# Weight sums of the down projection kept in a DRAM scratch in a one-layer decoder step

## The chip, the cores and the metric
One core of one Trainium2 chip runs the whole program. The metric is the device time of one execution in microseconds (us), lower is better. The engines are TensorE (PE in the profile), VectorE (DVE), ScalarE (ACT), GpSimd (POOL) and SyncE (SP), which issues all the DMA transfers named here.

## The reference, cut to what matters
```python
def _layer(x, ...):                       # 1024 prompt + 64 sample tokens, D_MODEL = 1024
    ...                                   # input projection, attention, S5, output projection
    h = x + mixed
    hn = rmsnorm(h, norm2_g)
    y = h + (jax.nn.silu(hn @ w_gate) * (hn @ w_up)) @ w_down    # D_FF = 2816, float32
    return y, ...
```
A final RMSNorm with `final_norm_g` follows. The change concerns the last product, with `w_down` (2816 x 1024).

## The kernel before, in words
All 1088 tokens go through one layer. The last third of the time is the feed-forward block (`phase_e`): first gate and up (`ffn`), then the down projection (`down`). Tokens lie in two halves `t` of 2 x 272 columns.

Float32 products are made from two parts of each operand: `split` (L63 to L65) writes the high part with ACT (L64) and the rest, source minus high part, with DVE (L65) or, for some tiles, with POOL. `mm3` (L68 to L72) then does three matmuls of 128x128 weights on 272 columns.

Both stages use Strassen's scheme with seven products `j` for each 2x2 block, and so sums of weight blocks. In gate and up a step is one product for both token halves, 8 groups of three matmuls; from its second group of columns on there are 140 such steps. `wsums` (L1615) makes three of the weight sums on POOL when a unit's weights have landed, `wpart` (L1624) a fourth at j = 3; `wsplit` then splits the 128x512 block for the step, LA = 3 steps ahead of its product, into a ring `ws` of 5 buffers.

In `down` a unit is (t, d, u): token half, 256 output columns, and a third of the 2816 rows. Units u = 0 and 1 have seven Strassen steps of 12 matmuls, u = 2 has six steps of plain products, whose one difference is made in `sums` (L1755). So each (t, d) has 20 steps, and there are 160 in all. `load(i)` fetches the raw weights of the next unit at its predecessor's first step, `sums(i + 1)` makes its sums on POOL at the third step. Both token halves use the same weights: they are loaded and summed twice. The hidden activations come back from DRAM (`hs<-dH`, `xp<-dH`, in `fill` and `plain`) and are split as well: 14 tiles of 128x1088 and four of 128x816 at the start of each token half, one per step (`cut`). Further work of POOL here: the base sums (L1794) and the scaling of finished rows (L1887).

The order on each engine's queue is worked out when the program is built, by a scheduler that goes by readiness and program order; on the chip each queue then runs in that fixed order. Loads and stores all stand in SP's queue.

Of the kernel before, what the change touches and what calls it, by code (L numbers as in the profile page):

```python
# [10 lines left out]
F32 = mybir.dt.float32  # L11
# [3 lines left out]
OP = mybir.AluOpType  # L15
# [31 lines left out]
class K:  # L47
# [1286 lines left out]
    def phase_e(self):  # L1334
        nc, I, O = self.nc, self.I, self.O
        V = nc.vector
        with ExitStack() as st:
# [4 lines left out]
            wp = E(self.pool("wpE", 1))  # L1342
# [21 lines left out]

            dH = [[self.dram.tile([7, 128, 4, HW] if u < 2 else [4, 128, 3, HW], F32, name=f"dH{t}{u}") for u in range(3)] for t in range(2)]
            dy = [self.dram.tile([2 * HW, 1024], F32, name=f"dy{t}") for t in range(2)]
            fs = ExitStack()
            fh = fs.enter_context(self.pool("fh", 1))
            fz = fs.enter_context(self.pool("fz", 1))
# [215 lines left out]

            self.cuts, self.step = [], 0
            HS = {}
            for step in ffn:
                self.cut()
                for s in step:  # L1590
                    self.fill(HS, dH, hnew, 0, *s)
                next(side, None)
# [31 lines left out]
    def wpart(self, R, S, j):  # L1624
        (a, b), (s1, s2) = R, S
        if j == 3:
            self.nc.gpsimd.tensor_tensor(out=s2, in0=b[:, :, 0:128], in1=s2, op=OP.subtract)  # L1627
        return (a[:, :, 0:128], s2, b[:, :, 0:128], a[:, :, 128:256], s1, s2, b[:, :, 128:256])[j]


    def ffn(self, wp, fp, X, dH, wraw, wsplit, htile, stile, ttile):
        nc, I = self.nc, self.I
        V, G = nc.vector, nc.gpsimd
        P = NF // 2
        mats = [(p, m, (t,)) for p in (0,) for t in range(2) for m in "gu"]
        mats += [(p, m, (0, 1)) for p in range(1, P) for m in "gu"]
        R, S, W = {}, {}, {}

        def load(i):
            if i < len(mats):  # L1640
                p, m, _ = mats[i]
                w = I["ffn_w_gate" if m == "g" else "ffn_w_up"][0][:, 256 * p:256 * p + 256].rearrange("(k p) c -> p k c", p=128)
                R[i] = [wraw(), wraw()]
                for h in range(2):
                    self.load(R[i][h], w[:, 4 * h:4 * h + 4])

        def sums(i):
            if i < len(mats):
                S[i] = self.wsums(wp, R[i], 4)

        def prep(n):
            i, j = divmod(n, 7)
            if i < len(mats):
                W[n] = wsplit(self.wpart(R[i], S[i], j))
        load(0)
        yield
        sums(0)
        load(1)
        yield
        for n in range(LA):  # L1660
            prep(n)
        yield
        yield
        st, hid = {}, {}
        for n in range(7 * len(mats)):
            i, j = divmod(n, 7)
            p, m, tps = mats[i]
            if j == 0:
                load(i + 1) if i else None
            elif j == 2:  # L1670
                sums(i + 1)
            prep(n + LA)
            for t in tps:
                z = st.setdefault((i, t), {})
                z[j] = self.bank("mm")[:, :HW]
                x = X[t][XN[j]]
                for kt in range(4):
                    self.mm3(z[j], W[n][:, 0, kt], W[n][:, 1, kt], x[:, 0, kt], x[:, 1, kt], kt == 0, kt == 3)
                if j == 0:
                    z["r"] = ttile("t1", "r")  # L1680
                    nc.scalar.activation(z["r"], z[0], AF.Copy)
                    continue
                if j == 1:
                    z["u2"] = ttile("t2", "u2")
                    V.tensor_tensor(z["u2"], z["r"], z[1], op=OP.add)
                    continue
                if j == 3:
                    z["u3"] = ttile("t3", "u3")
                    V.tensor_tensor(z["u3"], z["u2"], z[3], op=OP.add)
                    continue  # L1690
                if j == 2:
                    z["s" if m == "g" else "o"] = stile() if m == "g" else htile("hid")
                s = z["s"] if m == "g" else st[i - 1, t]["s"]

                mt, tt = {2: (0, 0), 4: (1, 1), 5: (0, 1), 6: (1, 0)}[j]
                sb = s[:, 2 * mt + tt]
                o = sb if m == "g" else z["o"][:, mt, HW * tt:HW * tt + HW]
                u = {2: z["r"], 4: z.get("u3"), 5: z.get("u4"), 6: z.get("u3")}[j]
                V.tensor_tensor(o, u, z[j], op=OP.subtract if j == 6 else OP.add)  # L1699
                if j == 4:  # L1700
                    z["u4"] = ttile("t1", "u4")
                    V.tensor_tensor(z["u4"], z["u2"], z[4], op=OP.add)
                if m == "g":
                    nc.scalar.activation(sb, sb, AF.Silu)
                    continue
                G.tensor_tensor(out=o, in0=o, in1=sb, op=OP.mult)  # L1706
                strassen = p < 8
                ob = z["o"].rearrange("p m (c t) -> p (m c) t", c=2)
                if j == 5 and strassen:
                    z["x"] = htile("x").rearrange("p m (c t) -> p (m c) t", c=2)  # L1710
                    for out, b, c in ((z["x"][:, 0], 1, ob[:, 0]), (z["x"][:, 1], 3, z["x"][:, 0]), (ob[:, 1], 3, ob[:, 1])):
                        G.tensor_tensor(out=out, in0=ob[:, b], in1=c, op=OP.subtract)
                if j == 6:
                    d = dH[t][p // 4][:, :, p % 4].rearrange("a p t -> p a t")
                    self.store(d[:, 0:4], ob)
                    if strassen:
                        G.tensor_tensor(out=z["x"][:, 2], in0=ob[:, 2], in1=z["x"][:, 1], op=OP.subtract)
                        self.store(d[:, 4:7], z["x"][:, 0:3])
            yield [(0, j)] + [(1, k) for k in range(7) if j == 6] if p == P - 1 and m == "u" else ()
# [4 lines left out]
    def down(self, wp, dp, HS, dh, dH, dy, wraw, wsplit, hnew):  # L1724
# [2 lines left out]
        wd = I["ffn_w_down"][0]  # L1727
        units = [(t, d, u) for t in range(2) for d in range(4) for u in range(3)]
        steps = [(i, j) for i in range(len(units)) for j in range(7 if units[i][2] < 2 else 6)]
        R, S, W, HO, GF = {}, {}, {}, {}, {}  # L1730
        SS = [dp.tile([128, 6, 4 + t], F32, name=f"ss{t}") for t in range(2)]
        G.memset(SS[1], 1.0)

        def load(i):
            if i < len(units):
                t, d, u = units[i]
                n = 4 if u < 2 else 3
                w = wd[1024 * u:1024 * u + 256 * n, 256 * d:256 * d + 256].rearrange("(q h p) c -> h p q c", h=2, p=128)
                R[i] = [wraw()[:, :n] for h in range(2)]
                for h in range(2):  # L1740
                    self.load(R[i][h], w[h])
                if u == 1:
                    HO[t, d] = self.dpx[2].tile([128, 2, 2 * HW], F32, tag="o", name="o", bufs=2)
                    self.load(HO[t, d], dh[t][d].rearrange("a p t -> p a t"))
                    GF[t, d] = dp.tile([128, 256], F32, tag="gf", name="gf", bufs=1)
                    self.load(GF[t, d], I["final_norm_g"].unsqueeze(0)[:, 256 * d:256 * d + 256].to_broadcast((128, 256)))

        def sums(i):
            if i < len(units):
                if units[i][2] < 2:  # L1750
                    S[i] = self.wsums(wp, R[i], 4)
                else:
                    S[i] = [wp.tile([128, 4, 128], F32, tag="st", name="st", bufs=2)[:, :3] for h in range(2)]
                    for h in range(2):
                        G.tensor_tensor(out=S[i][h], in0=R[i][h][:, :, 0:128], in1=R[i][h][:, :, 128:256], op=OP.subtract)  # L1755

        def prep(n):
            if n < len(steps):
                i, j = steps[n]
                if units[i][2] < 2:  # L1760
                    W[n] = wsplit(self.wpart(R[i], S[i], j))
                else:
                    w, h = divmod(j, 2)
                    W[n] = wsplit(S[i][h] if w == 2 else R[i][h][:, :, 128 * w:128 * w + 128], 3)

        def plain(t, c):
            for h in range(2):
# [2 lines left out]
                self.cuts.append((self.step, x[:, 0], x[:, 1], raw(x[:, 1]), G if (h, c) in PPOOL else None))  # L1770
        tail = iter(())
        load(0)
        for c in range(2):
            plain(0, c)
        sums(0)
        for n in range(LA):
            prep(n)
        for n, (i, j) in enumerate(steps):
            t, d, u = units[i]
            if j == 0:  # L1780
                load(i + 1)
                if u == 0:
                    z = {k: self.bank("mm")[:, :HW] for k in (0, 1, 3, 2, 4, 6, 5)}
            elif j == 2:
                sums(i + 1)
            prep(n + LA)
            self.cut()
            next(tail, None)
# [187 lines left out]
```

## Time and profile before
| | |
|---|---|
| median of 3 runs | 1586.97 us (1584.7 to 1587.9) |
| profiled execution | 1586.99 us, span 1585.2 us |
| busy: PE, DVE, POOL, ACT | 1451.3, 1156.9, 890.2, 718.1 us |
| gate and up, steady part | about 900 to 1276 us of the span |
| down projection | about 1276 to 1572 us of the span |

Times in rows are us from the span's start, unless ns is written. A busy PE is not PE at its peak; the number of matmuls in a stretch tells how fast it went. A time behind an instruction holds all that it waits for once it has started.

### The profile page before, as it was taken

The numbers are of one execution on the slowest core, as the hardware profiler recorded it, in microseconds if no ns is written. First come the engines' busy times: TensorE is split into PE (matmuls) and PEld (weight loads), VectorE is DVE, ScalarE is ACT, GpSimd is POOL, SyncE is SP. The second block draws the span as 40 slices with busy tenths as digits, with TensorE's granted clock in tenths as the row PEclk, the third lists the DMA queues.
The fourth block names the chain that finished last, engine by engine and source line by source line (L and its number), as shares of the span: only waits on it lengthen the run. The fifth ranks groups of instructions, "written<-read, shape, count | busy, mean of one in ns | idle before, by whom it ended". The sixth has DMA issues, their size and how long they took to land.

```text
span 1585.2 us, 27784 instructions
## 1 busy us (share of the span) xinstructions
PE 1451.3 (92%) x9909; PEld 1348.1 (85%) x9909; DVE 1156.9 (73%) x2178; ACT 718.1 (45%) x1831; POOL 890.2 (56%) x807
## 2 busy tenths in 40 slices
PE   6988988889999999899869999999999989988896
PEld 5978978867777677789859999999999979977896
DVE  6895489858757777688898555555555597799685
ACT  6233434345476766764444323233333453454343
POOL 3069445337635465555678656555553395678672
PEclk9998988859669999799989999999999999999998
DMA  8438888697775762633314332223332473384654
GB/s 218 155 132 286 239 245 228 195 230 191 200 199 162 200 180 80 177 99 109 110 40 129 104 103 91 83 88 89 92 102 82 147 269 122 127 305 142 185 156 121
DMA packets 213464, 246.20 MB, mean 155 GB/s; under 512 B 26798, under 2 KB 164878, under 8 KB 213326
## 3 DMA queue, kind: packets, MB, share of 16 engines
q1 hardware_dynamic: 213326, 244.43, 52.4%
q8 instruction: 78, 1.28, 0.4%
q14 instruction: 60, 0.49, 0.1%
HBM read 184.43 MB, written 59.95 MB: 154 GB/s over the span
## 4 chain that ended last, share of the span: by engine, by line
PE 58%; DVE 21%; DMA 8%; issue 5%; POOL 3%; ACT 3%; SPq 1%; DVEq 0%; POOLq 0%; ACTq 0%
PE pmm L72 14%; PE pmm L70 14%; PE pmm L71 14%; PE psd L75 7%; PE pmm L75 4%; DVE ws L65 4%; PE ppo L75 2%; PE ptr L79 2%; DMA kk<-in_cache_attn_k_dram 2%; DVE hT L1545 1%; DVE hn L65 1%; DVE hs L65 1%; DVE kk L680 1%; DVE Sm L687 1%; DMA wr<-in_w_in_dram 1%
## 5 line engine op out<-in xcount | busy, mean ns | idle before, releaser
L70 PE MATMUL pmm<-hn,ws 128*128 128x272 f32 x1232 | 359.3, 292 | 9.3 <-DVE s L1699 6.4
L72 PE MATMUL pmm<-hn,ws 128*128 128x272 f32 x1232 | 358.2, 291 | 3.1 <-DVE ws L65 3.1
L71 PE MATMUL pmm<-hn,ws 128*128 128x272 f32 x1232 | 357.9, 291 | 2.5 <-DVE hn L65 2.5
L65 DVE TENSOR_TENSOR ws<-wr,ws 128x512 fp32r<-128x512 f32 (+2 forms) x240 | 258.1, 1084 | 35.4 <-ACT ws L64 34.7
L70 PEld LDWEIGHTS pmm<-hn,ws 128*128 128x128 f32 x1232 | 234.3, 190 | 10.2 <-issue 7.7
L71 PEld LDWEIGHTS pmm<-hn,ws 128*128 128x128 f32 x1232 | 234.6, 190 | 3.1 <-DVE hn L65 3.1
L72 PEld LDWEIGHTS pmm<-hn,ws 128*128 128x128 f32 x1232 | 234.0, 190 | 3.6 <-DVE ws L65 3.4
L64 ACT ACTIVATE ws<-wr 128x512 fp32r<-128x512 f32 (+2 forms) x240 | 152.2, 642 | 173.8 <-PE pmm L72 165.9
L65 DVE TENSOR_TENSOR ws<-st,ws 128x512 fp32r<-128x512 f32 (+1 forms) x136 | 132.2, 975 | 82.9 <-ACT ws L64 82.0
L64 ACT ACTIVATE ws<-st 128x512 fp32r<-128x512 f32 (+1 forms) x136 | 83.6, 616 | 134.4 <-PE pmm L72 98.5
L72 PE MATMUL pmm<-hs,ws 128*128 128x272 f32 x448 | 133.3, 298 | 8.6 <-DVE ws L65 7.9
L70 PE MATMUL pmm<-hs,ws 128*128 128x272 f32 x448 | 132.4, 296 | 4.6 <-DVE hid L1699 4.3
L71 PE MATMUL pmm<-hs,ws 128*128 128x272 f32 x448 | 132.0, 295 | 0.1
L1619 POOL TENSOR_TENSOR st<-wr 128x512 f32<-128x512 f32 x40 | 56.7, 1417 | 102.0 <-DVE ws L65 101.2
L1706 POOL TENSOR_TENSOR hid<-hid,s 128x272 f32<-128x272 f32 x88 | 82.0, 938 | 43.7 <-DVE hid L1699 43.7
L826 POOL TENSOR_TENSOR vs<-vr,vs 128x512 fp32r<-128x512 f32 x40 | 55.6, 1398 | 86.5 <-ACT vs L824 75.0
L1627 POOL TENSOR_TENSOR st<-wr,st 128x512 f32<-128x512 f32 x40 | 57.8, 1444 | 80.3 <-DVE ws L65 80.3
L679 POOL TENSOR_TENSOR kf<-kf,qb 128x1024 f32<-128x1024 f32 x24 | 61.5, 2570 | 67.6 <-DMA kf<-in_cache_attn_k_dram 54.4
L72 PEld LDWEIGHTS pmm<-hs,ws 128*128 128x128 f32 x448 | 85.9, 192 | 11.4 <-DVE ws L65 11.3
L70 PEld LDWEIGHTS pmm<-hs,ws 128*128 128x128 f32 x448 | 86.3, 193 | 5.2 <-issue 4.5
L71 PEld LDWEIGHTS pmm<-hs,ws 128*128 128x128 f32 x448 | 86.3, 193 | 0.3 <-DVE hs L65 0.3
L1123 DVE CUSTOM_DVE_ANT_0 P<-pmm,lnc 128x256 f32<-128x256 f32 (+1 forms) x128 | 47.6, 377 | 52.7 <-PE pmm L75 42.2
(438 smaller groups left out, 4193.8 us busy)
## 6 DMA issues: line engine op xcount, KB each, us to landing
vr<-in_cache_attn_v_dram SPq DMA_DIRECT2D x80, 256.0 KB
wr<-in_ffn_w_down_dram SPq DMA_DIRECT2D x32, 512.0 KB
hs<-dH SPq DMA_DIRECT2D x28, 544.0 KB
kf<-in_cache_attn_k_dram SPq DMA_DIRECT2D x48, 256.0 KB
wr<-in_ffn_w_gate_dram SPq DMA_DIRECT2D x24, 512.0 KB
wr<-in_ffn_w_up_dram SPq DMA_DIRECT2D x24, 512.0 KB
dH<-hid SPq DMA_DIRECT2D x22, 544.0 KB
wr<-in_w_in_dram SPq DMA_DIRECT2D x16, 512.0 KB
```

Of the source, the lines that this page charges most:

```text
L64: self.nc.scalar.activation(hi, src, AF.Copy)
L65: (eng or self.nc.vector).tensor_tensor(out=lo, in0=src, in1=raw(hi), op=OP.subtract)
L70: nc.tensor.matmul(out, lhsT=wh, rhs=xh, start=start, stop=False)
L71: nc.tensor.matmul(out, lhsT=wh, rhs=xl, start=False, stop=False)
L72: nc.tensor.matmul(out, lhsT=wl, rhs=xh, start=False, stop=stop)
L75: self.nc.tensor.matmul(out, lhsT=w, rhs=x, start=start, stop=stop)
L679: nc.gpsimd.tensor_tensor(out=kf[i], in0=kf[i], in1=qb[b][:, 0:1].to_broadcast((128, 2, 512)), op=OP.mult)
L826: eng.tensor_tensor(out=s[:, 1], in0=vr[i], in1=raw(s[:, 0]), op=OP.subtract)
L1123: V.tensor_tensor_reduce(out=P[h, g].rearrange("p b k -> p (b k)")[:, o:o + n], in0=s[:, o:o + n], in1=lnc[:, part, 256 - n:256], scale=-1 ...
L1619: G.tensor_tensor(out=s1, in0=a[:, :, 128:256], in1=b[:, :, 128:256], op=OP.add)
L1627: self.nc.gpsimd.tensor_tensor(out=s2, in0=b[:, :, 0:128], in1=s2, op=OP.subtract)
L1706: G.tensor_tensor(out=o, in0=o, in1=sb, op=OP.mult)
```

## The change
The seven (or, for u = 2, six) weight blocks of each unit are made once, before `down`, and kept in four DRAM tensors `dS`, one for each `d`. A generator `stationary` does it in 24 pieces, two for each (u, d). A piece loads its raw weights in four loads of 128x256 (u = 2: two), makes its sums on POOL with four instructions of 128x256 (u = 2: one of 128x384), and stores them with four stores (u = 2: two). A piece is traced at every fifth step of gate and up from step 39 to step 154, and its POOL instructions are placed behind `self.mark`, the last product `hid` made on POOL so far. In `down`, `load`, `sums` and `wpart` no longer touch weights; `wload(k)` reads the finished blocks of two steps (4 KB for each partition where both are Strassen steps) in one load, six pairs ahead, into a ring of seven buffers (four of the old `wr`, three new `wx`).

```diff
+            self.dS = [self.dram.tile([128, 74, 128], F32, name=f"dS{d}") for d in range(4)]
...
-            for step in ffn:
+            dwp = fs.enter_context(self.pool("dw", 1))
+            stat = self.stationary(dwp)
+            for n, step in enumerate(ffn):
                 self.cut()
+                if n > 35 and n % 5 == 4:
+                    with self.tc.issue_after(self.mark):
+                        next(stat, None)
...
+    def stationary(self, dw):
...
+        for u in range(3):
+            for d in range(4):
+                o = self.dS[d]
+                for x in range(2):
+                    R = dw.tile([128, 2, 2, 2, 128], F32, tag="dr", name="dr", bufs=2)
+                    S = dw.tile([128, 3, 2, 128], F32, tag="ds", name="ds", bufs=2)
+                    if u == 2:
...
+                        for k in range(2):
+                            self.load(R[:, 3 * k:3 * k + 3], w[x, k])
+                        G.tensor_tensor(out=S, in0=R[:, 0:3], in1=R[:, 3:6], op=OP.subtract)
+                        o2 = o[:, 56:74].rearrange("p (w h q) c -> p w h q c", w=3, h=2)
+                        self.store(o2[:, 0:2, x], R.rearrange("p (w q) c -> p w q c", w=2))
+                        self.store(o2[:, 2, x], S)
+                    else:
...
+                        for h in range(2):
+                            for k in range(2):
+                                self.load(R[:, h, k], w[h, k])
+                        G.tensor_tensor(out=S[:, 1], in0=R[:, 0, 1], in1=R[:, 1, 1], op=OP.add)
+                        G.tensor_tensor(out=S[:, 0], in0=S[:, 1], in1=R[:, 0, 0], op=OP.subtract)
+                        G.tensor_tensor(out=S[:, 2], in0=R[:, 1, 0], in1=S[:, 0], op=OP.subtract)
+                        G.tensor_tensor(out=R[:, 0, 1], in0=R[:, 0, 0], in1=R[:, 0, 1], op=OP.subtract)
+                        o7 = o[:, 28 * u:28 * u + 28].rearrange("p (j q) c -> p j q c", q=4)[:, :, 2 * x:2 * x + 2]
+                        self.store(o7[:, 0:4:3], R[:, 0])
+                        self.store(o7[:, 2:7:4], R[:, 1])
+                        self.store(o7[:, 1], S[:, 0])
+                        self.store(o7[:, 4:6], S[:, 1:3])
+                    yield
...
-                G.tensor_tensor(out=o, in0=o, in1=sb, op=OP.mult)
+                self.mark = G.tensor_tensor(out=o, in0=o, in1=sb, op=OP.mult).ins
...
-                R[i] = [wraw()[:, :n] for h in range(2)]
-                for h in range(2):
-                    self.load(R[i][h], w[h])
...
-        def sums(i):
-            if i < len(units):
-                if units[i][2] < 2:
-                    S[i] = self.wsums(wp, R[i], 4)
-                else:
-                    S[i] = [wp.tile([128, 4, 128], F32, tag="st", name="st", bufs=2)[:, :3] for h in range(2)]
-                    for h in range(2):
-                        G.tensor_tensor(out=S[i][h], in0=R[i][h][:, :, 0:128], in1=R[i][h][:, :, 128:256], op=OP.subtract)
+        def place(n):
+            k, j = divmod(n, 20)
+            return k % 4, 4 * j if j < 14 else 14 + 3 * j
+        def wload(k):
+            if 2 * k < len(steps):
+                d, a = place(2 * k)
+                b = place(2 * k + 1)[1] + (4 if k % 10 < 7 else 3)
+                R[k] = (dp.tile([128, 8, 128], F32, tag="wx", name="wx", bufs=3) if k % 7 > 3 else wraw().rearrange("p a (b c) -> p (a b) c", b=2))[:, :b - a]
+                self.load(R[k], self.dS[d][:, a:b])
 
         def prep(n):
             if n < len(steps):
-                i, j = steps[n]
-                if units[i][2] < 2:
-                    W[n] = wsplit(self.wpart(R[i], S[i], j))
-                else:
-                    w, h = divmod(j, 2)
-                    W[n] = wsplit(S[i][h] if w == 2 else R[i][h][:, :, 128 * w:128 * w + 128], 3)
+                if n % 2 == 0:
+                    wload(n // 2 + 6)
+                m = 4 if n % 20 < 14 else 3
+                W[n] = wsplit(R[n // 2][:, m * (n % 2):m * (n % 2) + m], m)
...
         load(0)
+        for k in range(2):
+            wload(k)
         for c in range(2):
             plain(0, c)
-        sums(0)
+        for k in range(2, 6):
+            wload(k)
```

## Rows read from the trace of the kernel before

**Rows 1.** Windows: length, then each engine's busy us (instructions), clock, DMA share, GB/s.
```profile
1000.00:1100.00 100.00, 100.00 (x796) 100.00 (x795) 55.41 (x98) 31.07 (x61) 54.06 (x54) 1.00 0.30 93
1100.00:1200.00 100.00, 100.00 (x796) 100.00 (x795) 56.47 (x99) 30.73 (x60) 57.07 (x58) 1.00 0.32 99
```
**Rows 2.** Windows of down, same columns: PE, PEld, DVE, ACT, POOL.
```profile
1268.00:1314.00 46.00, 37.22 (x250) 35.08 (x250) 45.39 (x42) 23.99 (x34) 41.62 (x24) 0.90 0.67 244
1314.00:1388.00 74.00, 74.00 (x578) 73.99 (x577) 55.33 (x78) 33.08 (x73) 43.01 (x33) 0.97 0.40 127
...
1482.00:1571.00 89.00, 88.16 (x694) 87.98 (x695) 65.85 (x99) 39.55 (x101) 53.93 (x39) 0.98 0.51 153
...
1388.00:1482.00 94.00, 75.69 (x557) 71.28 (x556) 84.19 (x91) 45.83 (x89) 74.67 (x45) 0.98 0.65 215
```
**Rows 3.** What PE waited for, 1240 to 1330: total us, times, longest.
```profile
PE pmm L70 <- DVE hid L1699: 4.3, 1, 4.3
PE pmm L72 <- DVE ws L65: 3.4, 4, 1.1
```
**Rows 4.** What PE waited for, 1384 to 1484.
```profile
PE pmm L72 <- DVE ws L65: 10.2, 10, 3.0
PE ptr L79 <- ACT junk L1875: 8.3, 6, 3.7
```
**Rows 5.** Timeline of DVE and POOL, five single instructions: start, us, what.
```profile
1183.21 0.69 DVE L65 TENSOR_TENSOR ws<-st,ws 128x512 fp32r<-128x512 f32 x1 [0.29 <-ACT ws L64]
...
1395.06 1.29 DVE L65 TENSOR_TENSOR hs<-hs 128x1088 fp32r<-128x1088 f32 x1 [2.86 <-ACT hs L64]
...
1406.89 3.00 DVE L65 TENSOR_TENSOR ws<-wr,ws 128x512 fp32r<-128x512 f32 x1
...
1405.78 3.56 POOL L65 TENSOR_TENSOR hs<-hs 128x1088 fp32r<-128x1088 f32 x1
...
1061.62 0.78 POOL L1712 TENSOR_TENSOR x<-hid 128x272 f32<-128x272 f32 x1
```
**Rows 6.** POOL's instructions on `wr`, the weight sums, by stretch: length, busy.
```profile
1268.00:1314.00 46.00, 11.85 (x8) 0.90 0.67 244
1314.00:1388.00 74.00, 33.56 (x24) 0.97 0.40 127
1388.00:1482.00 94.00, 34.54 (x23) 0.98 0.65 215
1482.00:1571.00 89.00, 30.72 (x23) 0.98 0.51 153
```
**Rows 7.** DVE's splits by form, 1388 to 1482, and one from 1268 to 1314.
```profile
L65 DVE TENSOR_TENSOR ws<-wr,ws 128x512 fp32r<-128x512 f32 x17 | 21.3, 1262 | 0.0
L65 DVE TENSOR_TENSOR ws<-st,ws 128x512 fp32r<-128x512 f32 x14 | 20.1, 1435 | 2.3 <-ACT ws L64 2.2
L65 DVE TENSOR_TENSOR hs<-hs 128x1088 fp32r<-128x1088 f32 x8 | 16.1, 2009 | 3.6 <-ACT hs L64 3.6
L65 DVE TENSOR_TENSOR ws<-wr,ws 128x384 fp32r<-128x384 f32 x8 | 11.7, 1483 | 0.0
L65 DVE TENSOR_TENSOR ws<-st,ws 128x384 fp32r<-128x384 f32 x4 | 5.0, 1266 | 0.0
...
L65 DVE TENSOR_TENSOR xpFalse<-xpFalse 128x816 fp32r<-128x816 f32 x2 | 2.0, 1002 | 0.0
...
L65 DVE TENSOR_TENSOR ws<-st,ws 128x384 fp32r<-128x384 f32 x2 | 1.0, 545 | 0.0
```
**Rows 8.** DVE's splits (L65), 1268 to 1314: length, busy.
```profile
1268.00:1314.00 46.00, 41.67 (x30) 0.90 0.67 244
```
**Rows 9.** What ACT and SP waited for in gate and up, 900 to 1230.
```profile
ACT ws L64 <- PE pmm L72: 162.8, 93, 2.4
ACT s L1704 <- DVE s L1699: 36.5, 32, 1.7
ACT r L1681 <- PE pmm L72: 26.8, 30, 1.1
...
SPq L82 <- DVE ws L65: 253.7, 25, 12.1
```
**Rows 10.** POOL's costliest group of sums in gate and up, by form, 900 to 1230.
```profile
L1627 POOL TENSOR_TENSOR st<-wr,st 128x512 f32<-128x512 f32 x16 | 20.9, 1303 | 53.0 <-DVE ws L65 53.0
```
**Rows 11.** DMA, 1388 to 1482: all bytes, queue's share, weight loads.
```profile
DMA packets 11579, 20.22 MB, mean 215 GB/s; under 512 B 836, under 2 KB 8292, under 8 KB 11572
...
q1 hardware_dynamic: 11572, 20.12, 64.0%
...
wr<-in_ffn_w_down_dram SPq DMA_DIRECT2D x8, 512.0 KB
wr<-in_ffn_w_down_dram SPq DMA_DIRECT2D x5, 384.0 KB
```
**Rows 12.** What ACT waited for, 1384 to 1484.
```profile
ACT ws L64 <- POOL st L1627: 5.4, 3, 3.5
...
ACT hs L64 <- DMA hs<-dH: 2.5, 1, 2.5
```

More of the change, by code (lines that the diff above doesn't have):

```diff
@@ L1628, in wpart @@
         return (a[:, :, 0:128], s2, b[:, :, 0:128], a[:, :, 128:256], s1, s2, b[:, :, 128:256])[j]
+    def stationary(self, dw):
+        nc = self.nc
+        G = nc.gpsimd
+        wd = self.I["ffn_w_down"][0]
+        for u in range(3):
[5 more added lines that the diff above has]
+                    if u == 2:
+                        R, S = R.rearrange("p h w q c -> p (h w q) c")[:, 0:6], S.rearrange("p s q c -> p (s q) c")[:, 0:3]
+                        w = wd[2048:2816, 256 * d:256 * d + 256].rearrange("(q h p) (w c) -> h w p q c", h=2, p=128, w=2)
+                        for k in range(2):
[5 more added lines that the diff above has]
+                    else:
+                        r0 = 1024 * u + 512 * x
+                        w = wd[r0:r0 + 512, 256 * d:256 * d + 256].rearrange("(q h p) (w c) -> h w p q c", h=2, p=128, w=2)
+                        for h in range(2):
[11 more added lines that the diff above has]
+                    yield
@@ L1729, in down @@
         steps = [(i, j) for i in range(len(units)) for j in range(7 if units[i][2] < 2 else 6)]
-        R, S, W, HO, GF = {}, {}, {}, {}, {}
+        R, W, HO, GF = {}, {}, {}, {}
         SS = [dp.tile([128, 6, 4 + t], F32, name=f"ss{t}") for t in range(2)]
@@ L1736, in load @@
                 t, d, u = units[i]
-                n = 4 if u < 2 else 3
-                w = wd[1024 * u:1024 * u + 256 * n, 256 * d:256 * d + 256].rearrange("(q h p) c -> h p q c", h=2, p=128)
-                R[i] = [wraw()[:, :n] for h in range(2)]
-                for h in range(2):
-                    self.load(R[i][h], w[h])
                 if u == 1:
@@ L1783, in down @@
                     z = {k: self.bank("mm")[:, :HW] for k in (0, 1, 3, 2, 4, 6, 5)}
-            elif j == 2:
-                sums(i + 1)
             prep(n + LA)
```

## The prediction, made before the run
> **What bounds the kernel now.** I read first the windows of each engine's busy time, because they tell PE-bound stretches from others, then what PE waited for in the others, then the two engines that share that blame.
>
> In steady gate and up PE is busy all the time and starts 796 matmuls in 100 us, one per 0.1256 us [rows 1]; that is my price for a matmul at full clock. POOL and DVE are each busy little more than half of it. Nothing that only shortens POOL's or DVE's work can help there.
>
> In the down projection two stretches fall behind. From 1268 to 1314 us PE starts 250 matmuls, worth 250 x 0.1256 = 31.4 us, in 46 us: 14.6 us lost. From 1388 to 1482 us it starts 557, worth 70.0 us, in 94 us: 24.0 us lost. Between them, and after 1482, PE is busy for 74.0 of 74 and 88.2 of 89 us [rows 2]. The two stretches are the starts of the two token halves, where the hidden tiles come back and are split beside the weights. All that any change to the feed of `down` can win is thus 14.6 + 24.0 = 38.6 us. Part of the first loss is the clock: the granted mean is 0.90 there, so for some of it PE ran at 1.2 instead of 2.4 GHz, after it had stood still.
>
> There PE waits for DVE: for the splits of weights, and for ACT's `junk`, which itself comes after DVE's `y` [rows 3, 4]. DVE is busy 45.4 of 46 and 84.2 of 94 us, POOL 41.6 and 74.7 [rows 2].
>
> **Why DVE is slow there.** A DVE split of 128x512 takes 0.69 us with POOL idle and one of 128x1088 1.29 us. The split that started at 1406.89 took 3.00 us, ending at 1409.89: POOL's 128x1088 instruction had started before it and ended at 1409.34, so only about 0.55 us of it lay outside [rows 5]. DVE stood until POOL was through. Over the second stretch the splits by form sum to 77.2 us. Alone they would take 31 x 0.69 + 12 x 0.545 + 8 x 1.29 + 3 x 1.0 = 41.3 us, the last term for the three `xp` tiles [rows 5, 7]. So some 36 us, 46%, of DVE's split time there is waiting for POOL.
>
> The Trainium skill, SBUF - State Buffer, Who interferes with whom, says that a DVE instruction with two SBUF inputs contends with GpSimd's reads, and that one of the two then blocks for the whole instruction; the 3.00 us split agrees. Taken strictly it gives a larger gain than I forecast, the third rival below.
>
> **The change, part by part.**
>
> *Sums taken off POOL in down.* 80 instructions go (four for each of 16 units, two for each of 8). They hold POOL for 11.9 us of the first stretch and 34.5 us of the second [rows 6]. In the second, that is 34.5 / 74.7 = 46% of POOL's time. If DVE's waiting shrinks in proportion, 36 x 0.46 = 16.6 us of DVE time come free. As DVE already had some idle time and POOL's remaining work (hidden tiles, base sums, output rows) moves closer together, I take 15. Bounds: 0, if the rest of POOL's work keeps DVE as late as now, and 24.0, when PE itself is the limit. In the first stretch 11.9 / 41.6 = 28% of POOL's time goes; DVE's 41.7 us of splits there [rows 8] at the same 46% hold 19 us of waiting, and 28% of that is 5. Bounds 0 and 14.6. In the other two stretches 33.6 and 30.7 us of sums go from POOL [rows 6], and PE has nothing to gain: zero, and by PE's 0.8 us of idle at most one.
>
> ACT also waited 5.4 us for the fourth sum (L1627) in the second stretch [rows 12]; that wait cannot come back, as blocks arrive finished. I count it within the 15.
>
> *Sums put on POOL in gate and up.* 16 x 4 = 64 instructions of 128x256 and 8 of 128x384. A 128x272 one takes 0.78 us [rows 5], a 128x512 one 1.30 [rows 10], so by the line between them 0.75 and 1.02: 56 us in all, 3.0 us for a piece of four. Pieces come every five steps, 5 x 24 x 0.1256 = 15 us apart. POOL is idle 43 to 46 us of 100, that is 6.5 us of 15 [rows 1], so it becomes about three quarters busy. What hides it: the splits in this stage wait for PE to free a `ws` buffer, 162.8 us in all, and ACT's other waits there are for DVE and PE, none for POOL [rows 9]; POOL itself waits 53.0 us for the splits before the fourth sum [rows 10]. Weights are split three steps of 24 matmuls ahead, 3 x 24 x 0.1256 = 9 us. DVE's splits will be blocked more often, with 40 us of 100 to spare. I take a loss of 2 us for the whole; bounds 0 and the second rival.
>
> *DMA in gate and up.* A piece of u = 0 or 1 loads 0.5 MB and stores 0.9 MB, in all about 31 MB over 24 x 15 us, 86 GB/s beside 93 to 99 at a share of 0.30 to 0.32 [rows 1]. Even at the same cost per byte the share stays near 0.6. Its eight issues stand in SP's queue, among loads that wait up to 12.1 us for a free buffer [rows 9]; behind them wait the gate and up weights and the stores of `hid`. The rings of two let a piece's loads go out up to two pieces (30 us) early, so I count zero; without that cover it is the second rival.
>
> *DMA in down.* For each (t, d) the weights grow from 2816 x 256 x 4 bytes = 2.88 MB to 74 blocks of 64 KB = 4.85 MB, 15.7 MB more over the stage. The second stretch holds about (557 - 24 transposes) / 12 = 44 steps, so 44 / 20 x 1.97 = 4.3 MB on top of 20.2. Its queue now moves them in 0.64 x 94 = 60 us, 336 GB/s [rows 11]. 24.5 MB at that rate take 73 us; forecast length is 94 - 15 = 79. It fits, narrowly, and rows of 4 KB instead of 1 KB should not be worse. Six pairs of lead (12 steps, 18 us) instead of four steps cover a burst. I take zero; the bound is the first rival.
>
> **Sum.** -5 - 15 + 2 = -18 us against the profiled execution's 1586.99 us (its span is 1585.2, the rest lies around it), which equals the median of 1586.97: **1569 us**.
>
> **Rivals.**
>
> *DMA takes DVE's place in the second stretch.* Speaks for it: in the first half of the stretch all 14 hidden tiles come in, ACT stood 2.5 us for one of them with weight splits queued behind it [rows 12], and my sum leaves 6 us of 79 for the queue to be idle. If the extra bytes make the tiles late, the 15 us shrink to about 2, and the time is 1587 - 5 - 2 + 2 = 1582. Against it: the tiles are needed 20 steps after their load. Chance 0.20.
>
> *POOL waits for its own loads in gate and up* (the other side). If a piece's loads stand in SP's queue behind a load that waits 12.1 us, POOL, which goes in order, stands still at the piece, and the next sums and `hid` products with it. The cover is 9 us; what exceeds it costs PE, about 3 us a piece. It decides from 20 / 24 = 0.8 us a piece on. If half of the pieces pay 3 us: 1587 - 20 + 36 = 1603. Against it: loads can go two pieces ahead, and a piece's position is behind a product already made. Chance 0.12.
>
> *The block goes wholly.* If each microsecond of POOL taken away frees one of DVE, the sums alone (19 x 1.30 + 4 x 1.02 = 28.8 us in the second stretch, 6 x 1.30 + 2 x 1.02 = 9.8 in the first) exceed or approach what is lost: PE-bound in the second, -24, and -10 in the first: 1587 - 34 + 2 = 1555. This is the strict reading of the skill page named above. Against it: hidden tiles on POOL stay. Chance 0.10.
>
> *Nothing moves.* The start of a half is paced by what stays (14 hidden tiles split on ACT, DVE and POOL, and in the first stretch the 4.3 us in which PE waits for the last `hid` evacuation [rows 3]); within 3 us of 1587. Chance 0.09.
>
> **Chances and range.** Forecast 0.49 (1558 to 1577). A measurement of this kernel tells about 0.2%, 3 us, from no change. Faster: 0.49 + 0.10 + 0.17 of the DMA rival = 0.76. Same: 0.09 + 0.03 = 0.12. Slower 0.12. The range leaves out what lies beyond the full block and most of the slower case: 1556 to 1587.
>
> **What the profile after would show.** Right: no sums on POOL after 1277 us, and splits of 128x512 in the two stretches well under the 1.26 and 1.44 us they average now [rows 7]; the second stretch some 15 us shorter; PE still at about 796 matmuls per 100 us in gate and up. Wrong: ACT or DVE waiting for `hs<-dH` or for the blocks read back (DMA rival); POOL waiting for DMA, and PE idle, every five steps in gate and up (second rival); unchanged split means (nothing moves).

## The result, and the profile after

The changed kernel takes 1566.41 us (median; 1563.41 to 1571.08) beside 1585.84 us of the kernel before: ratio 0.9881, 95% interval 0.9846 to 0.9915. That is 19.4 us less; 18 were forecast, at 1569 us in a range of 1556 to 1587.

The windows of the profile after, with the columns of [rows 1, 2]; the stretches are laid at about the same work as before (2084 matmuls in the four of `down`, 2079 before), so they begin and end earlier:

```profile
1000.00:1100.00 100.00, 100.00 (x797) 100.00 (x795) 58.49 (x100) 30.54 (x62) 75.28 (x78) 1.00 0.62 192
1100.00:1200.00 100.00, 100.00 (x796) 100.00 (x795) 57.19 (x98) 30.09 (x59) 71.55 (x72) 1.00 0.57 176
...
1268.00:1310.00 42.00, 32.84 (x238) 32.21 (x238) 35.85 (x39) 24.31 (x33) 23.42 (x14) 0.90 0.96 339
1310.00:1384.00 74.00, 74.00 (x588) 73.96 (x588) 45.62 (x80) 33.74 (x75) 10.78 (x12) 0.99 0.65 190
1384.00:1461.00 77.00, 72.70 (x568) 70.78 (x567) 64.47 (x89) 47.35 (x88) 34.50 (x20) 1.00 0.87 302
1461.00:1552.00 91.00, 87.64 (x690) 87.14 (x689) 52.22 (x104) 38.74 (x101) 24.93 (x19) 0.98 0.67 202
```

Gate and up start as many matmuls as before, 796 in 100 us, although GpSimd went from 54 to 75 us busy and the DMA share from 0.30 to 0.62. The second stretch now holds 568 matmuls in 77 us, worth 568 x 0.1256 = 71.3 us: 5.7 us are lost there, where 24.0 were. The first loses 42 - 238 x 0.1256 = 12.1 us instead of 14.6, the last 91 - 690 x 0.1256 = 4.3 instead of 89 - 694 x 0.1256 = 1.8, and the one between them 0.1 instead of 74 - 578 x 0.1256 = 1.4. So 19.6 us less are lost in `down`; the span is 20.2 us shorter.

The matmuls of each stage show the same without any laying of stretches. Those on `hn` belong to gate and up, those on `hs` to `down`; first of before, then of after (min/median/max ns, first and last start us):

```profile
L70 PE MATMUL pmm<-hn,ws x1232: 283/289/567, 785.4 to 1275.6; 128*128 128x272 f32 x176
L70 PE MATMUL pmm<-hs,ws x448: 282/288/564, 1276.0 to 1561.0; 128*128 128x272 f32 x150
```
```profile
L70 PE MATMUL pmm<-hn,ws x1232: 283/289/567, 785.1 to 1275.4; 128*128 128x272 f32 x176
L70 PE MATMUL pmm<-hs,ws x448: 282/288/563, 1275.8 to 1541.0; 128*128 128x272 f32 x150
```

From first to last, gate and up take 490.2 and 490.3 us: the sums moved there cost nothing that shows. The matmuls on `hs` take 285.0 and 265.2, which is 19.8 us less.

VectorE's splits in the second stretch, 1384 to 1461 us, beside [rows 7]:

```profile
L65 DVE TENSOR_TENSOR ws<-wr,ws 128x512 fp32r<-128x512 f32 x18 | 15.8, 903 | 1.2 <-ACT ws L64 1.1
L65 DVE TENSOR_TENSOR ws<-wx,ws 128x512 fp32r<-128x512 f32 x15 | 14.2, 960 | 4.4 <-ACT ws L64 4.4
L65 DVE TENSOR_TENSOR hs<-hs 128x1088 fp32r<-128x1088 f32 x8 | 10.3, 1284 | 4.4 <-ACT hs L64 4.4
L65 DVE TENSOR_TENSOR ws<-wx,ws 128x384 fp32r<-128x384 f32 x6 | 5.5, 935 | 0.0
L65 DVE TENSOR_TENSOR ws<-wr,ws 128x384 fp32r<-128x384 f32 x6 | 5.4, 917 | 0.0
L65 DVE TENSOR_TENSOR xpTrue<-xpTrue 128x816 fp32r<-128x816 f32 x1 | 4.1, 4067 | 0.0
...
L65 DVE TENSOR_TENSOR xpFalse<-xpFalse 128x816 fp32r<-128x816 f32 x2 | 2.2, 1116 | 0.0
```

The 128x512 splits take 0.90 and 0.96 us on average instead of 1.26 and 1.44, the eight hidden tiles 1.28 instead of 2.01, as if alone. One tile, `xpTrue`, still took 4.07 us. In all they take 57.5 us; priced as in the prediction (33 x 0.69 + 12 x 0.545 + 8 x 1.29 + 3 x 1.0 = 42.6) 15 us of this is waiting, where 36 were. What PE waits for in all of `down`, 1270 to 1560 us:

```profile
PE pmm L70 <- DVE hid L1744: 6.3, 1, 6.3
PE ptr L79 <- ACT junk L1918: 5.7, 4, 3.1
PE pmm L72 <- DVE ws L65: 1.6, 2, 1.2
```

Waits for weight splits, 10.2 and 3.4 us in [rows 3, 4], are down to 1.6. The wait for the last `hid` evacuation grew from 4.3 to 6.3, and one wait for `junk` of 3.1 us comes at 1488, after both starts.

### The profile page after: what moved, and what is told of

It reads as the page before. It is cut to its first block, busy times and chain, and to the rows that moved or that the text cites. A ratio compares the mean times of both kernels' runs of the same rounds, so it can differ in the third digit from the quotient of the medians.

```text
span 1565.0 us, 28085 instructions
## 1 busy us (share of the span) xinstructions
PE 1445.4 (92%) x9909; PEld 1345.4 (86%) x9909; DVE 1112.1 (71%) x2178; ACT 718.1 (46%) x1831; POOL 835.6 (53%) x799
## 3 DMA queue, kind: packets, MB, share of 16 engines
q8 instruction: 78, 1.28, 0.3%
## 4 chain that ended last, share of the span: by engine, by line
PE 60%; DVE 12%; DMA 6%; issue 3%; ACT 2%; POOL 2%; SPq 1%; POOLq 0%; DVEq 0%; ACTq 0%
PE pmm L72 15%; PE pmm L70 15%; PE pmm L71 15%; PE psd L75 6%; PE pmm L75 4%; PE ptr L79 2%; PE ppo L75 2%; DMA kf<-in_cache_attn_k_dram 2%; DVE ws L65 2%; DVE hT L1547 1%; DVE hn L65 1%; SPq L82 1%; DVE kk L680 1%; DMA hs<-dH 1%; DMA vr<-in_cache_attn_v_dram 1%
## 5 line engine op out<-in xcount | busy, mean ns | idle before, releaser
L65 DVE TENSOR_TENSOR ws<-wr,ws 128x512 fp32r<-128x512 f32 (+2 forms) x238 | 229.0, 968 | 58.1 <-ACT ws L64 57.2
L65 DVE TENSOR_TENSOR ws<-st,ws 128x512 fp32r<-128x512 f32 x72 | 66.6, 927 | 70.0 <-ACT ws L64 69.9
L64 ACT ACTIVATE ws<-st 128x512 fp32r<-128x512 f32 x72 | 45.2, 628 | 87.0 <-PE pmm L72 51.3
L72 PE MATMUL pmm<-mT,ws 128*128 128x272 f32 x256 | 75.5, 298 | 4.4 <-DVE ws L65 4.4
L70 PE MATMUL pmm<-mT,ws 128*128 128x272 f32 x256 | 74.4, 301 | 1.9 <-ACT mT L64 1.9
```

The costliest lines, as they stand in the source:

```text
L64: self.nc.scalar.activation(hi, src, AF.Copy)
L65: (eng or self.nc.vector).tensor_tensor(out=lo, in0=src, in1=raw(hi), op=OP.subtract)
L70: nc.tensor.matmul(out, lhsT=wh, rhs=xh, start=start, stop=False)
L72: nc.tensor.matmul(out, lhsT=wl, rhs=xh, start=False, stop=stop)
```

## The experiments

Each ratio is to the kernel before, measured beside it; the changed kernel's is 0.9881, and 0.9896 when it was measured again. The intervals in brackets reach 0.3 to 0.5% to either side, 4 to 8 us, so a smaller effect is not told by the time alone.

**GpSimd's work put back, unread.**
```diff
                 W[n] = wsplit(R[n // 2][:, m * (n % 2):m * (n % 2) + m], m)
+                if n % 2:
+                    r = R[n // 2]
+                    G.tensor_tensor(out=r[:, 0:m], in0=r[:, 0:m], in1=r[:, m:2 * m], op=OP.subtract)
```


> The changed kernel, and in the down projection 80 idle subtractions of 128x512 (u = 2: 128x384) come back on GpSimd, one for each pair of blocks, on a buffer whose splits are done; nobody reads the result. Theory A (the gain is VectorE freed from GpSimd's sums): the two starts of the token halves grow again, in all by 12 to 24 us, to 1578 to 1590. Theory B (the gain is that finished weights lie ready earlier): nobody waits for these sums, so 1564 to 1569.

Measured: 1590.25 us, ratio 1.0017 (0.9988 to 1.0046). The whole gain is gone, though nobody reads these results and blocks arrive finished and early; ACT waits for no sum here either. Theory B falls.

**As much GpSimd time, but without reading.**
```diff
+                if n % 2:
+                    r = R[n // 2]
+                    G.memset(r[:, 0:2 * m], 0.0)
+                    G.memset(r[:, 0:2], 0.0)
```


> As the run with 80 idle subtractions, but with fills of the same place instead, two for each pair, about 1.3 us by the durations of the fills in the trace before: GpSimd is as busy, but reads nothing. If it is GpSimd's reads that block VectorE (theory A in its narrow form): 1564 to 1570, splits of 128x512 as in the changed kernel. If any busy GpSimd delays the start of a half, because its own queue is then late with hidden tiles and base sums: 1578 to 1590, as with the subtractions.

Measured: 1571.13 us, 0.9899 (0.9849 to 0.995), just above the first of the two ranges. The windows of the second stretch, first with subtractions, then with fills:

```profile
1384.00:1461.00 77.00, 63.63 (x467) 61.43 (x466) 72.83 (x77) 41.22 (x75) 60.83 (x34) 0.96 0.71 252
```
```profile
1384.00:1461.00 77.00, 69.94 (x528) 68.74 (x527) 63.31 (x89) 45.80 (x86) 58.90 (x64) 0.96 0.80 278
```

GpSimd is busy 60.8 and 58.9 us, nearly the same. VectorE is busy 72.8 us with subtractions and 63.3 with fills, 64.5 in the changed kernel; PE starts 467, 528 and 568 matmuls. VectorE's splits alone (L65; busy, number) with subtractions, with fills and in the changed kernel:

```profile
1384.00:1461.00 77.00, 66.27 (x50) 0.96 0.71 252
...
1384.00:1461.00 77.00, 54.64 (x54) 0.96 0.80 278
...
1384.00:1461.00 77.00, 56.16 (x56) 1.00 0.87 302
```

A split takes 1.33, 1.01 and 1.00 us on average. Priced by form as above, the three hold 30, 14 and 15 us of waiting. So it is GpSimd's reading of SBUF that makes VectorE stand, and not that GpSimd is busy. The matmuls on `hs`, with subtractions, then with fills, tell what that is worth in `down`:

```profile
L70 PE MATMUL pmm<-hs,ws x448: 283/289/563, 1272.5 to 1557.3; 128*128 128x272 f32 x150
...
L70 PE MATMUL pmm<-hs,ws x448: 283/289/567, 1277.2 to 1550.5; 128*128 128x272 f32 x150
```

From first to last these are 284.8 and 273.3 us, beside 285.0 before and 265.2 in the changed kernel. So the fills still cost 8 us in their profiled execution, which was the slowest of four (1576.62 us); by the medians they cost 0 to 5 us, inside the intervals. What they cost may be GpSimd's full queue; this was not tested.

**The lead of the read-back cut to that of before.**
```diff
-                    wload(n // 2 + 6)
+                    wload(n // 2 + 2)
...
-        for k in range(2, 6):
-            wload(k)
```


> The changed kernel with blocks read back two pairs ahead instead of six, which is the lead of the kernel before (four steps). Theory A: at most 5 us is lost, 1564 to 1572. Theory B (the early read is the gain): 1580 or more.

Measured: 1570.95 us, 0.9902 (0.987 to 0.9934). The deep prefetch is worth nothing that the intervals can tell.

**The kernel before without sums in `down`.** `sums` makes none, and each step splits a raw block of the unit in place of its sum, so the last product's weights are other ones.


> The kernel before, with the weight sums of the down projection left out (raw blocks are multiplied in their place): no GpSimd work for them anywhere, no scratch, loads and lead as before. Theory A: as fast as the changed kernel, 1560 to 1570, since its 15.7 MB of extra reads and the sums moved into gate and up cost nothing. Theory B: most of the gain needs the early read, so 1575 to 1587.

Measured: 1570.15 us, 0.9892 (0.9848 to 0.9936). No scratch, no extra bytes, no work moved, and the time is that of the changed kernel. So the scratch, 15.7 MB more reading and the pieces in gate and up together cost no more than the interval.

**Pieces in gate and up made twice and three times.**
```diff
+                        for _ in range(2):
+                            G.tensor_tensor(out=S[:, 1], in0=R[:, 0, 1], in1=R[:, 1, 1], op=OP.add)
+                            G.tensor_tensor(out=S[:, 0], in0=S[:, 1], in1=R[:, 0, 0], op=OP.subtract)
+                            G.tensor_tensor(out=S[:, 2], in0=R[:, 1, 0], in1=S[:, 0], op=OP.subtract)
                         G.tensor_tensor(out=S[:, 1], in0=R[:, 0, 1], in1=R[:, 1, 1], op=OP.add)
-                        G.tensor_tensor(out=S[:, 0], in0=S[:, 1], in1=R[:, 0, 0], op=OP.subtract)
-                        G.tensor_tensor(out=S[:, 2], in0=R[:, 1, 0], in1=S[:, 0], op=OP.subtract)
```
That makes eight instructions for a piece instead of four. The second run has `range(3)` and the addition behind the loop twice, which makes twelve.

> The changed kernel with each sum of a Strassen piece in gate and up made twice (eight GpSimd instructions of 128x256 for a piece, four more, about 3.5 us by their 0.83 to 0.98 us; the same results). If the sums there are free because GpSimd has idle time and a lead (GpSimd is busy 72 to 80 us of 100 now, so 3 to 4 us of 15 idle): within 5 us of the changed kernel, 1563 to 1572. If they are already at the edge (the second rival's place): 16 pieces at 2 us or more, 1598 and up.

> The changed kernel with each sum of a Strassen piece made three times (eight GpSimd instructions more for a piece, about 7 us of every 15). By GpSimd's idle time of 3 to 4 us of 15 this no longer fits: 3 to 4 us over for each of 16 pieces, of which the lead of 9 us hides some between pieces: 1590 to 1630. If the time stays within 5 us of the changed kernel, the idle time was no measure of the cover.

Measured: 1577.17 us, 0.9927 (0.99 to 0.9954), and 1592.3 us, 1.0022 (0.9994 to 1.0049). Windows of 900 to 1200 us, twice, then three times:

```profile
900.00:1200.00 300.00, 293.81 (x2314) 293.03 (x2313) 174.14 (x289) 87.96 (x181) 278.16 (x295) 0.99 0.60 186
```
```profile
900.00:1200.00 300.00, 285.43 (x2215) 284.60 (x2214) 181.09 (x278) 84.19 (x174) 294.00 (x320) 0.97 0.49 153
```

GpSimd is busy 278 and 294 of 300 us, and PE falls behind. The matmuls on `hn`, twice, then three times:

```profile
L70 PE MATMUL pmm<-hn,ws x1232: 282/289/596, 791.0 to 1289.7; 128*128 128x272 f32 x176
...
L70 PE MATMUL pmm<-hn,ws x1232: 283/289/593, 783.1 to 1296.9; 128*128 128x272 f32 x176
```

Gate and up take 498.7 and 513.8 us instead of 490.3. So twice the sums cost 8.4 us in the profile, some 0.5 for each of the 16 pieces, and three times 23.5, or 1.5 for each. By the ratios it is (0.9927 - 0.9881) x 1586 = 7 us and 22; the first of these two is not clear of the intervals by itself. The first expectation missed, between its two cases; the second came out at the low end. The cover is real and nearly used up.

**Pieces without the place behind `mark`.**
```diff
-                    with self.tc.issue_after(self.mark):
-                        next(stat, None)
+                    next(stat, None)
```


> The changed kernel with the pieces no longer placed behind the product of their step: the scheduler puts them where GpSimd is free by its own account. If the place within a step does not matter while GpSimd has slack: 1563 to 1571. If a piece ahead of the products delays hidden activations or the next sums beyond the lead: 1575 or more, with PE idle between 950 and 1250 us.

Measured: 1597.8 us, 1.0073 (1.0042 to 1.0104): slower than before the change. But it did not test the place within a step, as was meant. The pieces ran much earlier, from 779 to 972 us instead of 890 to 1236, and so at first where the hidden tiles for gate and up are still being made. What ACT waited for, 780 to 860 us, and then one instruction of GpSimd from its timeline:

```profile
ACT ws L64 <- POOL st L1626: 17.0, 2, 13.7
...
ACT hn L64 <- POOL s L1515: 6.4, 2, 5.2
```
```profile
809.04 11.56 POOL L1663 TENSOR_TENSOR ds<-dr 128x256 f32<-128x256 f32 x1 [1.25 <-DMA dr<-in_ffn_w_down_dram]
```

An addition that takes 0.72 us elsewhere held GpSimd for 11.56, with more piece instructions, the sums of gate and up and then the hidden tiles behind it, and PE waited 22.8 us at once for the split of a hidden tile (`ACT hn`). Between 820 and 840 us it started no matmul. The matmuls on `hn` run from 788.0 to 1302.0, 514.0 us or 23.7 more than in the changed kernel:

```profile
L70 PE MATMUL pmm<-hn,ws x1232: 283/289/594, 788.0 to 1302.0; 128*128 128x272 f32 x176
```

**The gains of the final norm loaded once** into four buffers, instead of per (t, d) into one.


> The changed kernel with the four slices of the final norm's gains loaded once into four buffers, instead of for each (t, d) into one. Theory: the 4.6 us that one stretch of the second token half is slower in the changed kernel (the steps from 1483 to 1503 us) is VectorE waiting for a reload of these gains, which stands in SP's queue behind the loads and stores of finished rows: 1560 to 1564. If the wait is for the queue as a whole (the rows' own loads come next in it), nothing moves: 1565 to 1568.

Measured: 1566.8 us, 0.9858 (0.9818 to 0.9898). In its profile the slow steps of the second half are gone, the 120 matmuls that took 20.8 us take 15.9 (by the start of every 120th matmul on `hs` or `xp`), but another 120 at the start of the half took 20.8 instead of 17.8. In the repeat of the changed kernel below, the first of these 120 took 18.3 instead of 20.8, so they vary without any edit. Inconclusive by itself.

**Hidden tiles split on VectorE alone; the same with the gains loaded once; the changed kernel again.**
```diff
-FPOOL, PPOOL, VPOOL, HSP = ((3,), (1, 3, 5), (1, 3, 5), (1, 3, 5)), ((0, 1),), (0, 2, 4, 6, 8), (1, 3, 5, 7)
+FPOOL, PPOOL, VPOOL, HSP = ((), (), (), ()), (), (0, 2, 4, 6, 8), (1, 3, 5, 7)
```


> The changed kernel with the 11 hidden tiles whose rest part GpSimd splits in the two starts moved to VectorE. A GpSimd split of 128x1088 takes 2.7 us and more, one on VectorE alone 1.29. If the two engines shut each other out, the start of a half needs about 1.4 us less for each of the tiles that it waits for: 3 to 8 us faster than the changed kernel in the same call. If GpSimd's share is real help (both working at once): 5 us or more slower.

> Hidden tiles on VectorE and the gains loaded once, on the changed kernel. If the two add up: 4 to 10 us faster than the changed kernel in the same call.

> The changed kernel again, without any edit, on the same chip as the two others: 0.985 to 0.992 of the kernel before.

Measured: 1555.03 us, 0.9795 (0.9757 to 0.9833); 1551.37 us, 0.977 (0.9736 to 0.9803); 1569.25 us, 0.9896 (0.9866 to 0.9926). Giving VectorE more work makes the kernel faster than the changed one: by 14 us in the first run and 18 in the second. The 4 us between these two are inside the intervals. The tiles moved are twelve by the trace, ten of 128x1088 and two of 128x816, and not eleven. The two stretches in the run with both edits, and VectorE's splits in the second:

```profile
1268.00:1310.00 42.00, 36.89 (x282) 36.70 (x281) 38.10 (x50) 28.13 (x37) 11.54 (x11) 0.96 0.99 367
...
1384.00:1461.00 77.00, 77.00 (x617) 76.78 (x616) 64.10 (x107) 51.44 (x98) 31.47 (x16) 1.00 0.93 329
```
```profile
L65 DVE TENSOR_TENSOR hs<-hs 128x1088 fp32r<-128x1088 f32 x14 | 18.1, 1300 | 3.1 <-ACT hs L64 2.9
L65 DVE TENSOR_TENSOR ws<-wr,ws 128x512 fp32r<-128x512 f32 x20 | 14.1, 721 | 2.0 <-ACT ws L64 2.0
```

Fourteen hidden tiles instead of eight, and VectorE is not busier than in the changed kernel (64.1 and 64.5 us): its 128x512 splits take 0.72 us, so it hardly stands. PE is busy for all of the second stretch. The first moves 367 GB/s at a DMA share of 0.99.

**The kernel before with hidden tiles on VectorE**, the same edit alone.


> The kernel before, with the 11 hidden tiles of GpSimd split on VectorE, and no other edit: the sums stay in the down projection. If the two engines shut each other out and the sum of their time sets the starts of the halves, this edit alone frees 11 x 1.4 = 15 us of that time: 1572 to 1583. If it needs the sums out of the way first (VectorE is full): no change or slower, 1584 to 1592.

Measured: 1575.64 us, 0.9909 (0.9874 to 0.9945): 13 us, where the change brings 18 to 19, by one line. The two add up: 13.1 and 18.4 (the changed kernel measured again) make 31.5, and the kernel with both gained 32.6.

## Why the prediction was right

*The bound.* Right: the gain lies in the two starts of the token halves (18.3 and 2.5 us). Gate and up did not move, and the other two stretches of `down` moved by 1.3 us less and 2.5 us more.

*DVE stands while POOL reads.* Right, and now shown: subtractions that nobody reads take the gain back and bring 30 us of waiting into the splits of the second stretch; fills that keep GpSimd as busy leave it at 14, as in the changed kernel. The Trainium skill, SBUF - State Buffer, Who interferes with whom, says that VectorE with two SBUF inputs contends with a GpSimd instruction that reads SBUF, and not with one that only writes it; the waiting in these two runs agrees.

*Sums off POOL in `down`, -15 and -5.* The second stretch was under-sized: 24.0 - 5.7 = 18.3 us. By proportion 16.6 us of VectorE's waiting should have gone; 36 - 15 = 21 went. The splits of hidden tiles on VectorE lost all of their waiting (1.28 us instead of 2.01), which proportion does not give; why is not shown. The first was over-sized, 14.6 - 12.1 = 2.5 us: POOL's work there is mostly hidden tiles and `hid` products, which stay, and the 6.3 us wait for the last `hid` evacuation stays with them. The DMA share of 0.96 there was not yet the limit: with hidden tiles off GpSimd (and the gains loaded once) the share was 0.99, and the first 240 matmuls of `down` took 37.2 us instead of 43.2. That the two came to 20.8 for 20 is luck: one term was 3.3 us too small, the other 2.5 too large. ACT's wait of 5.4 us for the fourth sum rightly got no term of its own: with idle subtractions it is gone as well, and the gain with it.

*Sums on POOL in gate and up, +2.* It was 0: 490.3 us instead of 490.2. Two of the four 128x256 sums took 0.74 us (median), as priced at 0.75, but the third took 0.96 and the 128x384 ones 1.46 instead of 1.02, so a piece of four held GpSimd for 3.5 us on average and not 3.0. The argument (splits wait for PE's buffers, not for POOL) held, but with less in hand than I thought: at twice the work PE begins to wait. And ACT did wait for POOL in the changed kernel, which it did not before:

```profile
ACT ws L64 <- PE pmm L72: 131.8, 63, 2.4
...
ACT ws L64 <- POOL st L1627: 26.5, 7, 4.3
```

Those are seven waits of up to 4.3 us in 900 to 1230. PE shows no wait there, so the three-step lead covered them.

*DMA, 0.* Right. The second stretch moved 23.22 MB with the queue at 86% of 77 us, 66 us, so about 350 GB/s and not 336:

```profile
DMA packets 7983, 23.22 MB, mean 302 GB/s; under 512 B 892, under 2 KB 2170, under 8 KB 7975
...
q1 hardware_dynamic: 7975, 23.12, 86.1%
```

The run without sums and without extra bytes is no faster. In the changed kernel ACT waited 3.0 us for hidden tiles from DRAM in this stretch, little more than the 2.5 of before. So the first rival falls, but the faster runs come near it (share 0.99 and 0.93).

*The second rival* did not come: in the changed kernel POOL waited 0.6 us in all for a piece's loads. Of the two reasons given against it, the place behind a product already made is the one that a run tested: without the mark the pieces move 110 to 260 us forward, and the change is a loss. What cost most there was another mechanism than the rival's, a GpSimd that was held up and hidden tiles that came late behind its queue; waits of pieces for their loads were 13.6 us in eight, and the one ahead of the 11.56 us was 1.25.

*The measurement* tells less than the 3 us that the chances assumed: its interval for this change is 0.9846 to 0.9915, some 5.5 us to either side.

*Not foreseen:* 2.5 us come back after the second start. VectorE, in order, stood for 3.8 us at 1486 before a product with the gains, whose load stood in SP's queue behind a row's load. The profile names nobody for this gap; with the gains loaded once it is not there. That it makes up the 2.5 us is not shown, as the time of that run is inside the intervals.

## What to carry to other kernels

Where VectorE instructions with two SBUF operands meet GpSimd instructions that read SBUF, do not count on the two engines working side by side. In these kernels, work taken off GpSimd was worth about what VectorE waited for it, and tiles "shared out" to a GpSimd that needs 2.7 us for what VectorE does in 1.29 made both kernels slower, by 13 and 14 us. When work without near dependences goes into an earlier stage, look where the scheduler puts it: left alone it put it 110 to 260 us earlier, which cost 23.7 us of gate and up, where the pinned place cost none. No third place was tried.

## What the hardware showed that was not expected

GpSimd can be held up for much longer than one instruction of VectorE: in the run without the mark its 0.72 us addition took 11.56 us, from 809.04 to 820.60. VectorE ran without a gap until 820.36, its own instructions at the lengths they have alone (0.68 us for 128x512). What VectorE ran in the middle and at the end of it:

```profile
812.27 0.68 DVE L65 TENSOR_TENSOR ws<-st,ws 128x512 fp32r<-128x512 f32 x1
812.87 0.71 DVE L65 TENSOR_TENSOR hn<-hT,hn 128x544 fp32r<-128x544 f32 x1
813.50 0.68 DVE L65 TENSOR_TENSOR ws<-st,ws 128x512 fp32r<-128x512 f32 x1
814.11 0.42 DVE L1729 TENSOR_TENSOR u<-r,pmm 128x272 f32<-128x272 f32 x1
...
816.64 3.38 DVE L1547 SCALAR_TENSOR_TENSOR hT<-hT,g,rb 128x272 f32<-128x272 f32 x8
819.94 0.42 DVE L1733 TENSOR_TENSOR u<-u,pmm 128x272 f32<-128x272 f32 x1
```

The addition's end less its 0.72 us is 819.88: it seems to have got in when VectorE came to its last instruction, which has one operand in PSUM. Such instructions before it, 0.42 us each at 814.11 and 815.69, did not let it in. The kernel before with hidden tiles on VectorE shows a second case, first GpSimd, then VectorE:

```profile
1388.85 5.28 POOL L1627 TENSOR_TENSOR st<-wr,st 128x512 f32<-128x512 f32 x1 [6.09 <-DVE ws L65]
...
1392.90 0.42 DVE L1873 TENSOR_TENSOR y<-ptr,gf 104x256 f32<-104x256 f32 x1
```

A sum of 1.30 us alone ended at 1394.13, so it seems to have started at 1392.83, again with an instruction of VectorE that has one operand in PSUM. In the second stretch of the kernel before it was VectorE that stood [rows 5]. What decides which of the two stands, these runs do not show.
